# Weight halves in the attention stages: low halves on VectorE, all high halves on ScalarE, none on GpSimd

## The chip, the cores and the metric

One NeuronCore of a Trainium2 chip runs the whole kernel. The metric is device time in microseconds (us): the median of three runs, 1567.07 us for the kernel before (1562.07 to 1567.22). One execution was also profiled, and it took 1567.67 us, of which the profile's span covers 1564.4 us.

The engines carry the names of the profile. PE is TensorE (matrix products), DVE is VectorE, ACT is ScalarE, POOL is GpSimd and SP issues the loads. Each engine works through its own queue in order. An instruction that waits holds up all that stands behind it on its engine, and nothing on the others unless they need its result.

## The reference, cut to what matters

Three blocks run one after the other on a sequence of 512 tokens (16 more in front in the first block): a recurrent mixer with a gated MLP, the hybrid attention block with cross attention into 256 memory tokens, and a squared-ReLU MLP. The change touches the second block:

```python
def hybrid_mixer(h, w_in, g_group, sinks, w_out, rel_table):
    proj = (h @ w_in).astype(jnp.float32)
    ...
    ya = dilated_attention(heads(aq), heads(ak), heads(av), rel_table)
    yb = stick_breaking_attention(heads(bq), heads(bk), heads(bv))
    yc = sliding_window_sink_attention(heads(cq), heads(ck), heads(cv), sinks, rel_table)
    yd = moba_attention(heads(dq), heads(dk), heads(dv), rel_table)
    groups = []
    for y in (ya, yb, yc, yd):
        y = y.transpose(0, 2, 1, 3).reshape(B, S, -1)
        groups.append(y * lax.rsqrt(jnp.mean(y * y, axis=-1, keepdims=True) + NORM_EPS))
    y = jnp.concatenate(groups, axis=-1) * g_group.astype(jnp.float32)
    return y.astype(h.dtype) @ w_out
```

Four groups (A, B, C, D) of four heads with 64 features each share one input projection and one output projection. Behind them comes the cross attention with its own query, key, value and output weights.

## The kernel before, in words

The features stand on the 128 partitions and the tokens along the free axis. A product with fp32 accuracy is made from pairs: each operand is held as a high half and a low half in a reduced format, and PE makes three products (high with high, high with low, low with high). `weights` (line 112) fetches one 128x1024 piece of weights into the staging tile `wst` (SP queue, three buffers), makes the high half `whi` by a rounding copy, and makes the low half `wlo` by subtracting `whi` from `wst`. `whi` and `wlo` have three buffers each; the matmuls of lines 135 to 138, 165 to 168 and 1349 to 1352 read them. Each piece is asked for while the product in front of it is being made.

Who makes the halves is set by `self.wlow` and a counter `self.turns`. Over most of the kernel `wlow` is VectorE: ACT makes `whi` (line 125) and DVE makes `wlo` (line 126). In two places `wlow` is GpSimd: while the heads of the four groups are woven with the projections (line 1524 to 1527), and in the cross attention (line 1621 to 1717). There POOL makes every `wlo` (line 126), and `whi` is made in turns by DVE (line 123) and ACT (line 125).

The weave (line 1270) takes the heads as generators, advances them in turn and puts pieces of the projections between them. A head of group B makes scores (line 1231), masks its diagonal block on POOL (lines 1238 and 1252), splits on ACT and DVE (lines 106, 107, 1255, 1256) and multiplies into the values. The softmax heads of A, C and D make scores (1162), an exponential (1174), a scaling by the denominator (1180), transposes (1184) and a split from PSUM (106, 107). Queries and keys are evacuated on DVE (1354) and split by ACT and DVE (1119, 1120, 1131 to 1134). In the cross attention the residual `x` takes the output projection (1641), and `split_x` makes its halves on ACT (109) and DVE (110) and adds squares on POOL (241).

The order on each engine is not the order of the source: the framework's scheduler sets it when the program is built, from its own model of how long each instruction takes.

Of the kernel before, what the change touches and what calls it, by code (L numbers as in the profile page):

```python
# [11 lines left out]
FT = mybir.dt.float32  # L12
FR = mybir.dt.float32r
AF = mybir.ActivationFunctionType
OP = mybir.AluOpType
# [48 lines left out]
class Net:  # L64
    def __init__(self, ctx, tc, I, out, dump=None):
        self.ctx, self.tc, self.nc, self.I, self.out = ctx, tc, tc.nc, I, out
        self.dump = dump
        nc = self.nc
        ent = lambda name, bufs=1, space=None: ctx.enter_context(
            tc.tile_pool(name=name, bufs=bufs) if space is None else tc.tile_pool(name=name, bufs=bufs, space=space))  # L70
        self.const = ent("const")
        self.wst = ent("wst", 3)
        self.whi = ent("whi", 3)
        self.wlo = ent("wlo", 3)
        self.act = ent("act")
        self.nrm = ent("nrm")
        self.dram = ent("dram", 1, DR)
        self.pmx, self.turn, self.third = None, 0, 0
        self.wlow, self.turns = nc.vector, 0
        self.pmm = ent("pmm", 2, PS)  # L80

        c = self.const
        self.ident = c.tile([P, P], FT, name="ident")
        make_identity(nc, self.ident)
        self.ones = c.tile([P, P], FT, name="ones")
        nc.vector.memset(self.ones, 1.0)
        self.ones2 = c.tile([P, 2], FR, name="ones2")
        nc.vector.tensor_copy(self.ones2, self.ones[:, 0:2])
        self.eps = c.tile([P, 1], FT, name="eps")
        nc.vector.memset(self.eps, EPS)  # L90
        self.par = c.tile([P, NPAR], FT, name="par")
        nc.sync.dma_start(self.par, I["par"])
        self.tri = c.tile([P, P], FT, name="tri")
        nc.gpsimd.affine_select(self.tri, self.ones, pattern=[[1, P]], compare_op=OP.is_ge, fill=0.0, base=0,
                                channel_multiplier=-1)
# [16 lines left out]
    def weights(self, src, shape, own=None):  # L112

        nc = self.nc
        kt, cols = shape
        n = kt * cols
        st = self.wst.tile([P, 1024], FT, name="wst")
        nc.sync.dma_start(st[:, 0:n] if len(src.shape) == 2 else st[:, 0:n].rearrange("p (k c) -> p k c", k=src.shape[1]),
                          src)
        hi, lo = ((own or self.whi).tile([P, 1024], FR, name="whi"), (own or self.wlo).tile([P, 1024], FR, name="wlo"))  # L120
        self.turns += 1
        if self.wlow is nc.gpsimd and self.turns % 2:
            nc.vector.tensor_copy(hi[:, 0:n], st[:, 0:n])
        else:
            nc.scalar.activation(hi[:, 0:n], st[:, 0:n], AF.Copy)  # L125
        self.wlow.tensor_tensor(lo[:, 0:n], st[:, 0:n], hi[:, 0:n].bitcast(FT), OP.subtract)  # L126
        v = lambda t: t[:, 0:n].rearrange("p (k c) -> p k c", k=kt)
        return v(hi), v(lo)

# [1168 lines left out]
    def hybrid(self):  # L1298
        nc = self.nc
        V = nc.vector  # L1300
        I = self.I
        with ExitStack() as es:
# [129 lines left out]
            def heads(name, j):  # L1432
                def gens():
                    box = boxes[name]
                    g = "ABCD".index(name)
                    if name == "C":
                        yield from band_heads(j)
                        return
                    for i in range(2):
                        h = 2 * j + i  # L1440
                        y, yr, q = ys[2 * g + j], slice(64 * i, 64 * i + 64), box["q", j][i]
                        if name == "B":
                            yield from self.stick_units(q, box["k", j][i], box["v"], 64 * h, y, yr)
                            continue
                        e = self.bias_tile({"A": 0, "D": 8}[name] + h)
                        yield from self.softmax_units(lambda pair, q=q: (q, 256 * pair), box["k", j][i], box["v"],
                                                      64 * h, y, yr, causal, e)
                return gens
# [49 lines left out]
            def expand(jobs):  # L1498

                res = []  # L1500
                for job in jobs:
                    nxt = flat[order[id(job)] + 1:][:1]
                    steps = list(job[1])
                    if job is plan[0][1][-1]:
                        res += steps[:-1] + [lambda nx=nxt[0][0], s0=steps[-1]: (nx(), s0())]
                        continue
                    if nxt and nxt[0][0]:
                        s0 = steps[0]
                        steps[0] = lambda s0=s0, nx=nxt[0][0]: (nx(), s0())
                    res += steps  # L1510
                return res
# [9 lines left out]
            e3.close()  # L1521
            self.at = self.pool(e2, "at", 6)
            self.ap = self.pool(e2, "ap", 1)
            self.wlow = nc.gpsimd
            self.vx = self.pool(e2, "vx", 1)
            self.weave([(heads(*hs), expand(jobs)) for hs, jobs in plan[1:]])
            self.wlow = V
            if self.dump:
                for n in range(KT):
                    self.dump("y" + "ABCD"[n // 2], n % 2, ys[n])  # L1530
# [76 lines left out]
    def cross(self, es, out):  # L1607

        nc = self.nc
        V = nc.vector  # L1610
# [7 lines left out]
        self.qk = self.pool(es, "qk3", 6)  # L1618
        self.at = self.pool(es, "at3", 4)
        self.ap = self.pool(es, "ap3", 1)  # L1620
        self.wlow = nc.gpsimd
        self.me = self.pool(self.ctx, "mlpe", side="right")
        self.hid = []
        self.next_input(act2)
# [89 lines left out]
        for _, pieces in mups:  # L1714
            for piece in pieces[3:6]:
                piece()
        self.wlow = V

    def mlp_up(self, f, pool, tmp, ranges, own=None):

# [210 lines left out]
```

## Time and profile before

| what | value |
|---|---|
| median of the runs | 1567.07 us |
| the profiled execution / its span | 1567.67 us / 1564.4 us |
| PE busy | 1479.6 us (95%) |
| DVE busy | 1032.0 us (66%) |
| ACT busy | 724.1 us (46%) |
| POOL busy | 335.5 us (21%) |
| POOL on `wlo`, line 126 | 75.2 us, 34 instructions |

The shares are means over the whole span. The 34 `wlo` of POOL all lie between 876 and 1165 us, so a view of that stretch says more than the page: the busy time of each engine in it, the groups of instructions by line and shape with the mean time of one, the shortest, the middle and the longest instruction of a line, and the chain of waits, which goes back from the last instruction to what released each step.

### The profile page before, as it was taken

What the parts mean: (1) busy time and instruction counts of PE and PEld (TensorE: products, weight loads), DVE (VectorE), ACT (ScalarE), POOL (GpSimd) and SP (SyncE); (2) the same over time, 40 slices, a digit from 0 to 9 for tenths busy, and PEclk for the clock granted to TensorE, in tenths of its full rate; (3) what the DMA queues carried; (4) which work ended last, traced back from release to release, by engine and by line L of the source; (5) the groups of instructions that cost most, each with busy time, mean ns of one, the idle gap of its engine ahead of it and who ended that gap; (6) DMA issues with size and microseconds to landing.
All of it is one profiled execution on the core that took longest, in us unless ns stands there. A gap on an engine that the chain in (4) does not pass through costs nothing.

```text
span 1564.4 us, 25002 instructions
## 1 busy us (share of the span) xinstructions
PE 1479.6 (95%) x9761; PEld 1334.2 (85%) x9761; DVE 1032.0 (66%) x1968; ACT 724.1 (46%) x1400; POOL 335.5 (21%) x308
## 2 busy tenths in 40 slices
PE   5998999999989999999999999999789999999997
PEld 4988999988989899999999877877778888888886
DVE  8887879777577655555475878888887443344334
ACT  5233356664554433334455466575666431134332
POOL 4066721003342000000131445303342000000001
PEclk9998999999999999999999999999999999999998
DMA  5333232227444322223656222113220322333221
GB/s 189 96 98 105 80 120 75 64 74 234 148 136 135 95 93 93 90 95 118 187 152 217 78 67 68 55 44 125 90 81 32 93 95 93 96 94 96 93 94 54
DMA packets 66430, 161.95 MB, mean 104 GB/s; under 512 B 15100, under 2 KB 24556, under 8 KB 66184
## 3 DMA queue, kind: packets, MB, share of 16 engines
q1 hardware_dynamic: 64936, 157.74, 32.3%
q8 instruction: 76, 1.25, 0.3%
q0 software_dynamic: 288, 1.57, 0.3%
q10 hardware_dynamic: 1088, 1.05, 0.2%
q14 instruction: 42, 0.34, 0.1%
HBM read 153.92 MB, written 10.33 MB: 105 GB/s over the span
## 4 chain that ended last, share of the span: by engine, by line
PE 54%; DVE 10%; ACT 3%; issue 1%; DMA 1%; POOL 0%; DVEq 0%; ACTq 0%; POOLq 0%
PE mm L135 6%; PE mm L138 5%; PE mm L136 5%; PE mm L165 5%; PE mm L168 5%; PE mm L167 5%; PE mx L165 4%; PE mx L168 4%; PE mx L167 4%; DVE xl L110 2%; PE mx L135 2%; PE mx L138 2%; PE mx L136 2%; DVE ptl L107 1%; PE tr L1208 1%
## 5 line engine op out<-in xcount | busy, mean ns | idle before, releaser
L126 DVE TENSOR_TENSOR wlo<-wst,whi 128x1024 fp32r<-128x1024 f32 (+2 forms) x227 | 285.0, 1257 | 196.9 <-ACT whi L125 121.2
L125 ACT ACTIVATE whi<-wst 128x1024 fp32r<-128x1024 f32 (+3 forms) x244 | 251.9, 1034 | 302.9 <-PE mm L136 107.3
L168 PE MATMUL mm<-xl,whi 128*128 128x256 f32 (+4 forms) x808 | 233.5, 314 | 0.3 <-DVE xl L110 0.3
L167 PE MATMUL mm<-xh,whi 128*128 128x256 f32 (+4 forms) x808 | 233.1, 314 | 0.2 <-DVE x L1641 0.2
L167 PE MATMUL mx<-xh,whi 128*128 128x512 f32 (+4 forms) x552 | 170.6, 330 | 7.8 <-ACT xh L109 7.7
L168 PE MATMUL mx<-xl,whi 128*128 128x512 f32 (+4 forms) x552 | 170.9, 330 | 3.3 <-DVE xl L110 3.2
L167 PEld LDWEIGHTS mm<-xh,whi 128*128 128x128 f32 (+1 forms) x808 | 153.8, 190 | 9.9 <-DVE x L1670 0.3
L168 PEld LDWEIGHTS mm<-xl,whi 128*128 128x128 f32 (+1 forms) x808 | 153.3, 190 | 10.3 <-issue 0.6
L165 PE MATMUL mm<-xh,wlo 128*128 128x256 f32 (+4 forms) x808 | 139.2, 311 | 0.0
L135 PE MATMUL mm<-hh,whi 128*128 128x256 f32 (+1 forms) x496 | 139.2, 310 | 0.0
L136 PE MATMUL mm<-hl,whi 128*128 128x256 f32 (+1 forms) x496 | 139.0, 310 | 0.0
L165 PEld LDWEIGHTS mm<-xh,wlo 128*128 128x128 f32 (+1 forms) x808 | 116.4, 187 | 9.8 <-issue 0.5
L167 PEld LDWEIGHTS mx<-xh,whi 128*128 128x128 f32 (+1 forms) x552 | 105.8, 192 | 17.1 <-ACT xh L109 8.0
L168 PEld LDWEIGHTS mx<-xl,whi 128*128 128x128 f32 (+1 forms) x552 | 105.6, 191 | 14.3 <-DVE xl L110 4.9
L165 PE MATMUL mx<-xh,wlo 128*128 128x512 f32 (+4 forms) x552 | 104.6, 331 | 0.0
L126 POOL TENSOR_TENSOR wlo<-wst,whi 128x1024 fp32r<-128x1024 f32 (+1 forms) x34 | 75.2, 2217 | 120.5 <-PE mm L138 38.2
L993 POOL TENSOR_TENSOR acc<-acc,osq 128x256 f32<-128x256 f32 (+1 forms) x26 | 25.2, 969 | 344.6 <-ACT osq L990 344.6
L135 PEld LDWEIGHTS mm<-hh,whi 128*128 128x128 f32 x496 | 93.4, 188 | 6.1
L136 PEld LDWEIGHTS mm<-hl,whi 128*128 128x128 f32 x496 | 93.5, 189 | 5.8
L165 PEld LDWEIGHTS mx<-xh,wlo 128*128 128x128 f32 (+1 forms) x552 | 85.5, 193 | 9.4 <-issue 0.2
L138 PE MATMUL mm<-hh,wlo 128*128 128x256 f32 (+1 forms) x496 | 83.6, 310 | 1.9 <-DVE wlo L126 1.9
L138 PEld LDWEIGHTS mm<-hh,wlo 128*128 128x128 f32 x496 | 70.5, 188 | 8.0 <-DVE wlo L126 2.3
(553 smaller groups left out, 3353.3 us busy)
## 6 DMA issues: line engine op xcount, KB each, us to landing
wst<-in_w_in_dram SPq DMA_DIRECT2D x52, 512.0 KB, 3.6
wst<-in_w_down_dram SPq DMA_DIRECT2D x32, 512.0 KB, 3.5
wst<-in_w_mup_dram SPq DMA_DIRECT2D x32, 512.0 KB, 3.5
wst<-in_w_mdown_dram SPq DMA_DIRECT2D x32, 512.0 KB, 3.7
wst<-in_w_gate_dram SPq DMA_DIRECT2D x22, 512.0 KB, 3.5
wst<-in_w_up_dram SPq DMA_DIRECT2D x22, 512.0 KB, 3.6
wst<-in_w_out_dram SPq DMA_DIRECT2D x20, 512.0 KB, 3.6
wst<-in_w_down_dram SPq DMA_DIRECT2D x16, 384.0 KB, 3.5
```

Source lines behind the costliest of these rows:

```text
L107: nc.vector.tensor_tensor(lo, src, hi.bitcast(FT), OP.subtract)
L110: nc.vector.scalar_tensor_tensor(lo, src, gain, hi.bitcast(FT), OP.mult, OP.subtract)
L125: nc.scalar.activation(hi[:, 0:n], st[:, 0:n], AF.Copy)
L126: self.wlow.tensor_tensor(lo[:, 0:n], st[:, 0:n], hi[:, 0:n].bitcast(FT), OP.subtract)
L135: nc.tensor.matmul(ps, ah, bh, start=start and i == 0, stop=False)
L136: nc.tensor.matmul(ps, ah, bl, start=False, stop=False)
L138: nc.tensor.matmul(ps, al, bh, start=False, stop=stop and i == n - 1)
L165: nc.tensor.matmul(ps, wl[:, k], xh, start=False, stop=k == KT - 1)
L167: nc.tensor.matmul(ps, wh[:, k], xh, start=k == 0, stop=False)
L168: nc.tensor.matmul(ps, wh[:, k], xl, start=False, stop=False)
L993: nc.gpsimd.tensor_tensor(acc, acc, sq, OP.add)
L1208: nc.tensor.matmul(yp[0:64, c0:c1], m[:, j, vc:vc + 64], d[:, j - f0, c0:c1], start=ji == x == 0, stop=ji == len(jobs) - 1 and x == 2)
```

## The change

`self.wlow` and `self.turns` go. Everywhere in the kernel ACT makes `whi` and DVE makes `wlo`, as before the change outside of the two stretches. By the alternation 17 of the 34 `whi` of these stretches were made on DVE (13 of 1024 columns, 4 of 512); they move to ACT. The 34 `wlo` (26 of 1024 columns, 8 of 512) move from POOL to DVE.

```diff
@@ -76,7 +76,6 @@
         self.pmx, self.turn, self.third = None, 0, 0
-        self.wlow, self.turns = nc.vector, 0
         self.pmm = ent("pmm", 2, PS)
@@ -118,12 +117,8 @@
         hi, lo = ((own or self.whi).tile([P, 1024], FR, name="whi"), (own or self.wlo).tile([P, 1024], FR, name="wlo"))
-        self.turns += 1
-        if self.wlow is nc.gpsimd and self.turns % 2:
-            nc.vector.tensor_copy(hi[:, 0:n], st[:, 0:n])
-        else:
-            nc.scalar.activation(hi[:, 0:n], st[:, 0:n], AF.Copy)
-        self.wlow.tensor_tensor(lo[:, 0:n], st[:, 0:n], hi[:, 0:n].bitcast(FT), OP.subtract)
+        nc.scalar.activation(hi[:, 0:n], st[:, 0:n], AF.Copy)
+        nc.vector.tensor_tensor(lo[:, 0:n], st[:, 0:n], hi[:, 0:n].bitcast(FT), OP.subtract)
@@ -1521,10 +1516,8 @@
             self.ap = self.pool(e2, "ap", 1)
-            self.wlow = nc.gpsimd
             self.vx = self.pool(e2, "vx", 1)
             self.weave([(heads(*hs), expand(jobs)) for hs, jobs in plan[1:]])
-            self.wlow = V
@@ -1618,7 +1611,6 @@
         self.ap = self.pool(es, "ap3", 1)
-        self.wlow = nc.gpsimd
@@ -1714,7 +1706,6 @@
                 piece()
-        self.wlow = V
```

Line numbers of the changed kernel are 5 lower from line 126 on (line 126 becomes 121) and 8 lower in the cross attention (1641 becomes 1633).

The scheduler also moves other instructions. POOL's queue in the stage of the B heads, first before; `e` is a diagonal block of scores, masked by `strict`:

```order
L1238 TENSOR_TENSOR e_10463<-e_10463,strict_9967 128x128
L1252 TENSOR_TENSOR e_10484<-e_10484,strict_9967 128x128
L126 TENSOR_TENSOR wlo_10777<-wst_10774,whi_10776 128x1024
L1238 TENSOR_TENSOR e_10496<-e_10496,strict_9967 128x128
L126 TENSOR_TENSOR wlo_10931<-wst_10928,whi_10930 128x1024
L1252 TENSOR_TENSOR e_10526<-e_10526,strict_9967 128x128
```

The same place of POOL's queue in the changed kernel:

```order
L1233 TENSOR_TENSOR e_10463<-e_10463,strict_9967 128x128
L1247 TENSOR_TENSOR e_10484<-e_10484,strict_9967 128x128
L1233 TENSOR_TENSOR e_10496<-e_10496,strict_9967 128x128
L1247 TENSOR_TENSOR e_10526<-e_10526,strict_9967 128x128
L1233 TENSOR_TENSOR e_10540<-e_10540,strict_9967 128x128
```

The masks no longer stand behind a `wlo`. The two `wlo` of these rows are now in DVE's queue, here between pieces of the B heads (`ptl` is the low half of a block, `v2l` that of the values):

```order
L1232 SCALAR_TENSOR_TENSOR e_10496<-tr_10493,e_10496 128x512
L1251 TENSOR_TENSOR ptl0_10517<-e_10484,pth0_10516 128x256
L121 TENSOR_TENSOR wlo_10777<-wst_10774,whi_10776 128x1024
L109 SCALAR_TENSOR_TENSOR v2l_10409<-mm_10715,rc272_10186,v2h_10408 128x256
L121 TENSOR_TENSOR wlo_10931<-wst_10928,whi_10930 128x1024
L106 TENSOR_TENSOR ptl1_10400<-e_10496,pth1_10399 128x512
```

The `ptl1` of 512 columns now waits for both. The second place is the start of the cross attention on DVE, where `x` takes the output projection from PSUM. Before:

```order
L1641 TENSOR_TENSOR x0_5046<-x0_5046,mm_13154 128x256
L1641 TENSOR_TENSOR x1_5048<-x1_5048,mm_13171 128x256
L123 CAST whi_13217<-wst_13215 128x1024
L110 SCALAR_TENSOR_TENSOR xl0_13126<-x0_5046,par_89,xh0_13118 128x256
L123 CAST whi_13286<-wst_13284 128x1024
L110 SCALAR_TENSOR_TENSOR xl1_13127<-x1_5048,par_89,xh1_13119 128x256
L1641 TENSOR_TENSOR x2_5050<-x2_5050,mm_13196 128x256
L1641 TENSOR_TENSOR x3_5052<-x3_5052,mm_13221 128x256
```

The same place in the changed kernel:

```order
L1633 TENSOR_TENSOR x0_5046<-x0_5046,mm_13154 128x256
L1633 TENSOR_TENSOR x1_5048<-x1_5048,mm_13171 128x256
L109 SCALAR_TENSOR_TENSOR xl0_13126<-x0_5046,par_89,xh0_13118 128x256
L109 SCALAR_TENSOR_TENSOR xl1_13127<-x1_5048,par_89,xh1_13119 128x256
L1633 TENSOR_TENSOR x2_5050<-x2_5050,mm_13196 128x256
L121 TENSOR_TENSOR wlo_13218<-wst_13215,whi_13217 128x1024
L1633 TENSOR_TENSOR x3_5052<-x3_5052,mm_13221 128x256
L121 TENSOR_TENSOR wlo_13262<-wst_13259,whi_13261 128x1024
L121 TENSOR_TENSOR wlo_13287<-wst_13284,whi_13286 128x1024
L1633 TENSOR_TENSOR x4_5054<-x4_5054,mm_13240 128x256
```

Two `whi` went to ACT's queue and three `wlo` came in, of which two stand between the evacuations of `x3` and `x4`.

## Rows read from the trace of the kernel before

**Rows 1.** Busy time of each engine in a stretch (us from the span's start; length; busy us and instructions of PE, PEld, DVE, ACT, POOL; granted clock, DMA share, GB/s). The first stretch lies in the first block, where DVE makes the `wlo`; the second is the attention.

```profile
200.00:300.00 100.00, 100.00 (x816) 94.48 (x815) 85.50 (x170) 62.17 (x130) 15.38 (x17) 1.00 0.28 87
876.00:1200.00 324.00, 295.01 (x1930) 260.26 (x1929) 268.15 (x647) 201.61 (x534) 117.22 (x96) 0.98 0.22 71
```

**Rows 2.** POOL's groups by line and shape in 876 to 1200 us: count, busy us, mean ns of one, idle us of POOL just before them and what ended it.

```profile
L126 POOL TENSOR_TENSOR wlo<-wst,whi 128x1024 fp32r<-128x1024 f32 x26 | 64.4, 2480 | 61.0 <-PE tr L1208 24.1 <-ACT whi L125 16.0 <-DVE whi L123 6.2
...
L126 POOL TENSOR_TENSOR wlo<-wst,whi 128x512 fp32r<-128x512 f32 x8 | 10.8, 1361 | 59.5 <-PE mm L138 36.0 <-PE mm L1349 9.1 <-DVE qs L1120 7.1
```

**Rows 3.** Instructions of POOL and of DVE in order of time around 890 us: start us, us, engine, line.

```profile
890.13 2.59 POOL L126 TENSOR_TENSOR wlo<-wst,whi 128x1024 fp32r<-128x1024 f32 x1 [5.95 <-PE mm L1349]
...
888.71 0.68 DVE L1133 TENSOR_TENSOR kl<-qkn,kh 64x512 fp32r<-64x512 f32 x1 [0.37 <-ACT kh L1131]
...
890.93 2.33 DVE L1133 TENSOR_TENSOR kl<-qkn,kh 64x512 fp32r<-64x512 f32 x1
```

**Rows 4.** The low half of a block of scores, DVE line 107, read from PSUM (`tr`) and from SBUF (`e`), in 876 to 1165 us: shortest/middle/longest ns, first and last start.

```profile
L107 DVE TENSOR_TENSOR ptl<-tr,pth x53: 278/418/692, 1003.6 to 1164.8; 128x256 fp32r<-128x256 f32 x25, 128x128 fp32r<-128x128 f32 x12, 128x384 fp32r<-128x384 f32 x8, 128x512 fp32r<-128x512 f32 x8
L107 DVE TENSOR_TENSOR ptl<-e,pth x16: 292/558/2569, 904.5 to 985.7; 128x128 fp32r<-128x128 f32 x4, 128x256 fp32r<-128x256 f32 x4, 128x384 fp32r<-128x384 f32 x4, 128x512 fp32r<-128x512 f32 x4
```

**Rows 5.** DVE's groups by line and shape in 876 to 1200 us, as in rows 2.

```profile
L110 DVE SCALAR_TENSOR_TENSOR xl<-x,par,xh 128x256 fp32r<-128x256 f32 x33 | 27.6, 844 | 2.1 <-ACT xh L109 2.1
...
L1120 DVE TENSOR_TENSOR qs<-qkn,qs 64x512 fp32r<-64x512 f32 x16 | 13.1, 816 | 1.1 <-ACT qs L1119 0.6
L123 DVE CAST whi<-wst 128x1024 fp32r<-128x1024 f32 x13 | 12.3, 946 | 2.1 <-PE mm L136 2.1
L1133 DVE TENSOR_TENSOR kl<-qkn,kh 64x512 fp32r<-64x512 f32 x14 | 12.1, 866 | 3.0 <-ACT kh L1131 2.9
...
L126 DVE TENSOR_TENSOR wlo<-wst,whi 128x1024 fp32r<-128x1024 f32 x3 | 5.0, 1660 | 3.6 <-ACT whi L125 2.7 <-issue 0.8
L1256 DVE TENSOR_TENSOR ptl<-e,pth 128x512 fp32r<-128x512 f32 x4 | 5.0, 1239 | 0.1
```

**Rows 6.** Shortest/middle/longest ns of lines of DVE, as in rows 4; the row of line 126 is of the whole span (its list of shapes names three of more), and the last row says how long DVE sat idle before its 227 `wlo` until ACT's `whi` was there (us, times).

```profile
L110 DVE SCALAR_TENSOR_TENSOR xl<-x,par,xh x19: 469/774/2586, 875.4 to 1158.3; 128x256 fp32r<-128x256 f32 x19
L1133 DVE TENSOR_TENSOR kl<-qkn,kh x14: 674/689/2325, 888.7 to 1035.0; 64x512 fp32r<-64x512 f32 x14
L123 DVE CAST whi<-wst x17: 420/685/2897, 889.3 to 1160.8; 128x1024 fp32r<-128x1024 f32 x13, 128x512 fp32r<-128x512 f32 x4
L107 DVE TENSOR_TENSOR xl<-y,xh x6: 681/686/687, 1046.8 to 1103.3; 128x512 fp32r<-128x512 f32 x6
L1180 DVE TENSOR_SCALAR e<-e,den x8: 340/344/836, 1170.7 to 1182.7; 128x256 f32<-128x256 f32 x8
L1178 DVE TENSOR_TENSOR den<-den,es x16: 140/152/1459, 1065.1 to 1106.4; 128x1 f32<-128x1 f32 x16
L126 DVE TENSOR_TENSOR wlo<-wst,whi x227: 949/1225/2535, 6.9 to 1533.6; 128x1024 fp32r<-128x1024 f32 x105, 128x768 fp32r<-128x768 f32 x8, 128x64 fp32r<-128x64 f32 x1
...
  ACT whi L125: 121.2, 72
```

**Rows 7.** The chain of waits in 876 to 1200 us: start us, us, what. The first and the last of its 229 DVE pieces, and of the fourteen long ones among them six, the first and the last included.

```profile
887.58 0.44 DVE qkn L1354
...
890.93 2.34 DVE kl L1133
...
927.15 2.17 DVE ptl L107
...
1113.50 2.81 DVE whi L123
...
1118.09 4.13 DVE xl L110 x2
...
1155.21 2.54 DVE wlo L126
...
1161.64 2.73 DVE e L1180 x2
...
1184.65 1.33 DVE xl L110 x2
```

**Rows 8.** The first and the last of the 76 ACT pieces of the same chain.

```profile
887.16 0.39 ACT rs L294
...
1167.84 0.28 ACT pth L106
```

**Rows 9.** ACT's groups by line and shape in 876 to 1200 us, as in rows 2.

```profile
L125 ACT ACTIVATE whi<-wst 128x1024 fp32r<-128x1024 f32 x17 | 17.7, 1054 | 5.5 <-PE mm L138 4.0 <-PE mm L136 0.8 <-PE mm L1352 0.4
...
L125 ACT ACTIVATE whi<-wst 128x512 fp32r<-128x512 f32 x4 | 2.5, 630 | 2.7 <-POOL wlo L126 2.7
```

**Rows 10.** Who waited for whom in 876 to 1200 us: us in total, times, longest. The first and the last of the eight waits of PE for DVE, and one of ACT for POOL.

```profile
PE mm L135 <- DVE x L1641: 4.4, 4, 2.0
...
PE tr L1263 <- DVE ptl L1256: 1.0, 1, 1.0
...
ACT pth L106 <- POOL e L1238: 7.3, 10, 2.1
```

**Rows 11.** POOL's masks of the B heads and its sums of squares in 876 to 1200 us, shortest/middle/longest ns.

```profile
L1238 POOL TENSOR_TENSOR e<-e,strict x16: 455/540/969, 903.7 to 982.5; 128x128 f32<-128x128 f32 x16
...
L241 POOL TENSOR_TENSOR nacc<-nacc,sq x28: 727/778/1704, 875.3 to 1199.1; 128x256 f32<-128x256 f32 x28
```

## The prediction

> **What bounds the kernel now.** First comes the busy time by stretch [rows 1]. The change lies in the attention, 324 us from 876 to 1200 us. There PE is busy for 295.0 us, so it idles for 29.0 us, and DVE is busy for 268.2 us, or 83%. In the stretch of the first block PE is busy throughout, with DVE at 85.5% and DVE making the `wlo` there: a DVE that is this full need not stop PE.
>
> Then come POOL's groups [rows 2]. Its 34 `wlo` take 64.4 + 10.8 = 75.2 us, and POOL sits idle for 61.0 + 59.5 = 120.5 us before them. Read alone, this is an idle engine that takes work from a full one.
>
> The third view shows its price. At 890.13 us POOL begins a `wlo` of 2.59 us. A `kl` on DVE that begins at 890.93 takes 2.33 us and ends within 0.6 us of POOL's end, while the `kl` of the same form at 888.71 took 0.68 [rows 3]. Line 107 shows which instructions are hit: 53 that read one operand from PSUM never take over 0.69 us, and 16 of the same shapes that read both operands from SBUF take up to 2.57 [rows 4]. So a DVE instruction with two SBUF operands stands still while POOL makes a `wlo`. A cast from SBUF does too: at worst it takes 2.90 us and in the middle 0.69 [rows 6].
>
> The groups tell how much this is [rows 5, 6]: `xl` 27.6 - 33 x 0.47 = 12.1 us, `qs` 13.1 - 16 x 0.69 = 2.1, the cast 12.3 - 13 x 0.685 = 3.4, `kl` 12.1 - 14 x 0.69 = 2.4, `ptl` of 512 columns 5.0 - 4 x 0.69 = 2.2. That is 22 us in five groups alone, a few of them under POOL's smaller work.
>
> Last comes the chain of waits: 229 of its pieces in the attention are DVE's [rows 7], 123 us together, which is 46% of DVE's 268.2 busy. ACT has 76 pieces [rows 8] with 35.8 us, 18% of its 201.6.
>
> **The change part by part.** *The stall of DVE goes.* Fourteen DVE pieces of the chain between 890.93 and 1161.64 lie under a `wlo` of POOL and are over 1.3 us long [rows 7]; they add up to 34.2 us. Undisturbed, by the middle or shortest durations of rows 6, they are 0.69 each for one `kl`, one `qs`, five low or high halves of scores and one cast, 0.15 for a denominator, 0.47 for each of four `xl`, 1.23 for a `wlo` and 0.34 for each of two scalings, 9.5 together. Charging 0.69 for every half of scores, whatever its width, is on the safe side. So 34.2 - 9.5 = 24.7 us of stall stand on the chain. The bounds: 0, if another chain is always as late, and 29.0, all that PE idles [rows 1].
>
> *The low halves come to DVE.* 26 of 1024 columns at 1.225 us [rows 6] make 31.9 us, 8 of 512 columns at 0.686, as the `xl` of the same shape, make 5.5. The casts that leave are 13 x 0.685 + 4 x 0.42 = 10.6 us. Net, 37.4 - 10.6 = 26.8 us are added to DVE. On the path it is between 0 and all of it; I take DVE's share on the chain, 46%, since the new instructions stand between others of DVE: 12.3 us.
>
> *The high halves come to ACT.* 13 x 1.054 + 4 x 0.63 = 16.2 us [rows 9]. ACT is busy for 62% of the stretch; at its share of the chain, 18%, this is 2.9 us (bounds 0 and 16.2).
>
> *POOL's queue is shorter.* The masks of the B heads stood behind `wlo`, and ACT waited for them ten times, 7.3 us [rows 10]. At ACT's 18% this gives 1.3 us back (bounds 0 and 7.3). The loads of `xk` and `xv` that POOL issues also stand behind no `wlo` any more; I cost that at nothing. The staging buffers come free when DVE has read them, after 1.2 us and not 2.5, so SP can issue a load earlier; its queue moves a few loads of weights and bias past each other, and the rows name no wait for a load, so I cost this at nothing; a load that came late would cost its own lateness on the path.
>
> *New waits.* A `wlo` on DVE needs ACT's `whi`, the landed load and a free buffer. Behind it on DVE wait the evacuations and halves that follow, and PE for those; at the start of the cross attention two `wlo` stand between the evacuations of `x3` and `x4`. The casts that stood in the same places waited 2.1 us in all [rows 5], but a cast needs no other engine's half. I put nothing in the sum for it, and keep it as the first rival.
>
> The sum, against the profiled execution: 24.7 + 1.3 - 12.3 - 2.9 = 10.8 us less, 1567.67 - 10.8 = 1556.9. The median of the runs, 1567.07, is 0.6 lower than that execution, which doesn't matter here. I forecast 1557 us; for this case alone 1550 to 1564.
>
> A rule of the Trainium skill speaks against the change. Perfetto Trace Analysis, Optimizing Scalar/DVE Operations, says that with VectorE saturated it may make sense to give work to ScalarE or even GpSimd, and adds that between VectorE and GpSimd this might not help, as they share a read port. Its first half would have POOL's 75.2 us as a relief; this trace bears out the second half, with at least 22 us of stall in five groups, more than half of the 37.4 us that POOL takes over.
>
> **The rivals.** *DVE waits in line, slower.* POOL could afford to sit idle 120.5 us before its `wlo`; DVE can't. For it: in this kernel 72 of DVE's 227 `wlo` waited for ACT's `whi`, 121.2 us, 1.7 each [rows 6], and one of the three in this stretch waited 2.7 [rows 5]. Against it: those 72 are of the whole kernel and come to 0.5 us for each `wlo`, and the longest of POOL's waits were for PE (36.0 us for line 138 alone, rows 2), for buffers that a product frees with its end, whose evacuation now stands ahead of the `wlo` on DVE. If DVE inherits 48 us, two fifths, at 46% this costs 22 us: 1579. From 23 us on it eats up the gain, from 40 on the kernel is slower.
>
> *PE is right behind, no change.* The 24.7 us are stall on the chain, and it says nothing of the next latest. PE waited for DVE eight times in the list, 4.4 us down to 1.0, 18.2 together [rows 10]. If only these can shrink, then by the stall's share of the chain's DVE pieces, 24.7 of 123 or 20%, less the 10% that the net new work adds: 1.8 us, 1566. Against it: the chain goes through ACT and DVE in ways that PE's idle alone doesn't show.
>
> *More than the sum.* The stall off the chain counts too, and all 18.2 us of PE's waits for DVE go: 1549. For it speaks that all of the `wlo` work is shorter on DVE than the pair of POOL's work and stall; against it, that DVE stays at some 75%.
>
> *DVE now holds POOL up.* What reads two SBUF operands on DVE can also delay POOL: the longest mask takes 0.97 us and the shortest 0.46, the longest sum 1.70 and the shortest 0.73 [rows 11]. Some 13 of the new `wlo` stand among the B heads; at up to 1.23 us each this makes 16 us for the masks, and, at ACT's 18%, 2.9 us of the time: about 1560.
>
> Such a lock is what the Trainium skill states in SBUF — State Buffer, SBUF: two separate sides: of the two engines the one that starts first has the shared pair for its whole instruction and the other blocks. By that rule the stall would only change sides; the masks' and sums' longest times agree that POOL is held as well.
>
> **How the numbers follow.** The forecast has 0.46, the larger gain 0.11, PE right behind 0.17, the held POOL 0.07, DVE in line 0.19. About 0.5% is what can be told from no change here: 1559.2 to 1574.9. Of the forecast's 0.46, 0.36 lie below 1559.2, since the stalls under 1.3 us were not counted; with the larger gain faster has 0.47. The other 0.10, PE right behind and the held POOL make 0.34. Slower is the line on DVE, 0.19. The range has to leave 0.1 out on either side: below the larger gain's 1549 and into the upper half of the line on DVE, so 1547 to 1578.
>
> **What will show it.** In the attention POOL's busy time falls from 117 to about 42 us, and ACT's rises from 202 to about 218. The low halves of scores with both operands in SBUF no longer take over 1.2 us, and `xl` has a middle near 0.47. DVE's busy time doesn't rise though it has 26.8 us more to do; if it rises by that much, the stall was no stall. PE's idle of 29.0 us falls by some 10. The forecast is wrong if DVE's idle time before its new `wlo` comes to more than 23 us, or if PE's idle is the same in spite of a DVE that has become free.

## The result: 0.7% faster, and the profile after

The changed kernel takes 1553.45 us (median of 4 runs, 1551.67 to 1556.99) against 1566.24 us for the kernel before (4 runs): 0.9929 of its time, interval 0.9908 to 0.9949. Measured once more, later, the same kernel came to 0.9916 (0.9903 to 0.9928). The forecast was 1557 us, with 10.8 us of gain; by the first ratio it is 11 us, by the second 13.

The page of the changed kernel begins with the busy time of each engine, over the whole span:

```profile
span 1554.9 us, 24997 instructions
PE 1481.5 (95%) x9761; PEld 1337.3 (86%) x9761; DVE 1013.2 (65%) x1985; ACT 737.4 (47%) x1417; POOL 259.7 (17%) x274
```

In the kernel before, DVE was busy for 1032.0 us, 18.8 more, although by the prediction's count it has 26.8 us more to do now. Together that is some 45 us of stall that is gone, an estimate from these two numbers.

The attention as one stretch, as in [rows 1] (ten us shorter, since the kernel is):

```profile
876.00:1190.00 314.00, 295.02 (x1936) 261.24 (x1935) 250.99 (x665) 215.65 (x553) 42.59 (x64) 0.98 0.23 73
```

PE has the same 295.0 us to do and idles for 19.0 instead of 29.0. DVE's groups by line and shape in this stretch (count, busy us, mean ns, idle us before them and what ended it) answer to [rows 5]:

```profile
L121 DVE TENSOR_TENSOR wlo<-wst,whi 128x1024 fp32r<-128x1024 f32 x29 | 35.4, 1226 | 4.8 <-ACT whi L120 3.6 <-PE mm L1344 0.9
L109 DVE SCALAR_TENSOR_TENSOR xl<-x,par,xh 128x256 fp32r<-128x256 f32 x34 | 21.2, 633 | 1.1 <-ACT xh L108 1.0
...
L1115 DVE TENSOR_TENSOR qs<-qkn,qs 64x512 fp32r<-64x512 f32 x16 | 11.1, 696 | 1.9 <-ACT qs L1114 1.4
L1128 DVE TENSOR_TENSOR kl<-qkn,kh 64x512 fp32r<-64x512 f32 x14 | 9.6, 682 | 0.9 <-ACT kh L1126 0.6
```

The means of `qs` and `kl` fell from 816 and 866 ns to 696 and 682, which were the middle values before. Shortest, middle and longest of line 106 (107 before), of `xl` and of POOL's mask, to be read beside [rows 4], [rows 6] and [rows 11]:

```profile
L106 DVE TENSOR_TENSOR ptl<-e,pth x16: 280/488/694, 903.9 to 979.4; 128x128 fp32r<-128x128 f32 x4, 128x256 fp32r<-128x256 f32 x4, 128x384 fp32r<-128x384 f32 x4, 128x512 fp32r<-128x512 f32 x4
...
L109 DVE SCALAR_TENSOR_TENSOR xl<-x,par,xh x26: 468/582/958, 872.8 to 1164.3; 128x256 fp32r<-128x256 f32 x26
...
L1233 POOL TENSOR_TENSOR e<-e,strict x16: 458/463/975, 903.1 to 978.2; 128x128 f32<-128x128 f32 x16
```

A low half of scores with both operands in SBUF took up to 2569 ns before and takes at most 694 now. The middle `xl`, 582 ns, still stands above its undisturbed 0.47 us: POOL's sums of squares run beside it, and in a kernel below that makes these sums on DVE the middle is 477 ns.

Who waited for whom after the change (us in total, times, longest), as in [rows 10]:

```profile
ACT pth L105 <- POOL e L1233: 6.8, 7, 2.1
...
PE tr L1258 <- DVE pth L1250: 1.4, 1, 1.4
...
PE mm L130 <- DVE qkn L1349: 0.9, 1, 0.9
```

The first row is nearly that of before, 7.3 us. The other two come back below: they lie close together in one place, and there the kernel before waited too, 1.6 us for `qkn` and 1.0 for `ptl` (the last PE row of [rows 10]). The chain of waits of the same stretch, by line:

```profile
by line: PE mm L1347 8.1%; PE mm L1346 8.0%; PE mm L1344 8.0%; PE tr L1203 6.3%; PE mm L133 6.1%; PE mm L130 6.1%; PE mm L131 5.7%; PE sc L1157 3.4%; DVE xl L109 3.2%; PE tr L1179 3.0%; DVE wlo L121 2.4%; PE tr L1258 2.1%; DVE ptl L106 2.0%
```

The low halves are 2.4% of 314 us of chain, 7.5 us, out of 40.9 us (35.4 and eight of 512 columns) that they keep DVE busy. Over all lines the chain's DVE pieces add up to some 60 us; they were 123.

### The profile page after: what moved, and what is told of

Same layout as the page of the kernel before. It is cut to its first block, busy times and chain, and to the rows that moved or that the text cites. A ratio compares the mean times of both kernels' runs of the same rounds, so it can differ in the third digit from the quotient of the medians.

```text
span 1554.9 us, 24997 instructions
## 1 busy us (share of the span) xinstructions
PE 1481.5 (95%) x9761; PEld 1337.3 (86%) x9761; DVE 1013.2 (65%) x1985; ACT 737.4 (47%) x1417; POOL 259.7 (17%) x274
## 4 chain that ended last, share of the span: by engine, by line
PE 60%; DVE 6%; ACT 2%; DMA 1%; issue 0%; DVEq 0%; ACTq 0%
PE mm L130 6%; PE mm L133 6%; PE mm L131 6%; PE mm L160 5%; PE mm L163 5%; PE mm L162 5%; PE mx L160 4%; PE mx L163 4%; PE mx L162 4%; PE mx L130 2%; PE mx L133 2%; PE mx L131 2%; PE mm L1347 2%; PE mm L1346 2%; PE mm L1344 2%; PE tr L1203 1%
## 5 line engine op out<-in xcount | busy, mean ns | idle before, releaser
L121 DVE TENSOR_TENSOR wlo<-wst,whi 128x1024 fp32r<-128x1024 f32 (+2 forms) x261 | 320.9, 1231 | 201.4 <-ACT whi L120 122.6
L120 ACT ACTIVATE whi<-wst 128x1024 fp32r<-128x1024 f32 (+2 forms) x261 | 267.9, 1028 | 306.3 <-PE mm L131 114.7
L236 POOL TENSOR_TENSOR nacc<-nacc,sq 128x256 f32<-128x256 f32 (+2 forms) x62 | 59.9, 967 | 208.9 <-ACT sq L235 202.6
```

The lines of the kernel that those rows point to most:

```text
L121: nc.vector.tensor_tensor(lo[:, 0:n], st[:, 0:n], hi[:, 0:n].bitcast(FT), OP.subtract)
L236: (nc.vector if k % len(accs) else nc.gpsimd).tensor_tensor(acc[:, c:c + w], acc[:, c:c + w], sq, OP.add)
```

## The experiments

**One half of the change at a time.** In the first kernel DVE makes the low halves and the high halves go on in turns; in the second ACT makes all high halves and POOL keeps the low ones.

```diff
-        self.wlow.tensor_tensor(lo[:, 0:n], st[:, 0:n], hi[:, 0:n].bitcast(FT), OP.subtract)
+        nc.vector.tensor_tensor(lo[:, 0:n], st[:, 0:n], hi[:, 0:n].bitcast(FT), OP.subtract)
```

> Half of the change alone: all low halves on VectorE, the high halves in turns on VectorE and ScalarE as before. Theory A (the gain is the stall of VectorE under GpSimd's low halves, now gone): the casts stay, 10.6 us on VectorE at 46% cost 4.9 us against the changed kernel's 1553.5, ScalarE is spared 16.2 us at 18%, 2.9 us back: about 1555 us, nearly the whole gain. Rival B (the gain is the casts that left VectorE): 1562 to 1566 us, near the kernel before.

```diff
-        self.turns += 1
-        if self.wlow is nc.gpsimd and self.turns % 2:
-            nc.vector.tensor_copy(hi[:, 0:n], st[:, 0:n])
-        else:
-            nc.scalar.activation(hi[:, 0:n], st[:, 0:n], AF.Copy)
+        nc.scalar.activation(hi[:, 0:n], st[:, 0:n], AF.Copy)
```

> The other half alone: all high halves on ScalarE, the low halves of the attention stay on GpSimd. Theory A: the stall stays, the casts' 10.6 us leave VectorE (4.9 us less on the path) and 16.2 us come to ScalarE (2.9 more): about 1564 us, no change that can be told from before. The instructions of VectorE with two SBUF operands still take up to 2.5 us. Rival B: about 1555 us.

Low halves alone: 1550.08 us, 0.9899 (0.9880 to 0.9917). High halves alone: 1564.47, 0.9998 (0.9984 to 1.0012). The whole gain comes with the low halves. The page of the second kernel is the more telling one:

```profile
span 1561.7 us, 25004 instructions
PE 1479.5 (95%) x9761; PEld 1333.6 (85%) x9761; DVE 1013.8 (65%) x1951; ACT 737.1 (47%) x1417; POOL 331.5 (21%) x308
```

DVE and ACT are busy for the same time as in the changed kernel, within 0.6 us, and no gain can be told: here DVE's time still holds the stall, there it holds work that could wait. Line 107 in this kernel, `ptl<-e,pth`, still takes up to 1694 ns.

**POOL's work brought back as a ghost.** The changed kernel, with one instruction added behind each low half of the attention: POOL makes the same subtraction once more, in place in the staging tile, where nobody reads it. Once it is of full width, once of 64 columns. The two have the same instructions, but not the same order: from 913 us on, the scheduler gave DVE, ACT and PE their work in another sequence. So the pair compares POOL's time together with the order that was built around it; the expectation of the second ghost, written before, takes the places to be the same.

```diff
         nc.vector.tensor_tensor(lo[:, 0:n], st[:, 0:n], hi[:, 0:n].bitcast(FT), OP.subtract)
+        if self.ghost:
+            m = min(n, 1024)       # 64 in the second kernel
+            nc.gpsimd.tensor_tensor(st[:, 0:m], st[:, 0:m], hi[:, 0:m].bitcast(FT), OP.subtract)
```

> The changed kernel, and in the attention GpSimd makes each low half once more, in place in the staging tile, where nobody reads it (34 instructions of 1024 or 512 columns; the results are not touched). Theory A: GpSimd is busy for some 75 us more, VectorE's instructions with two SBUF operands again take up to 2.6 us, VectorE's busy time in the attention rises by some 45 us, and the time by the 24.7 us that were counted on the chain: about 1578 us, at least 1566, though nothing waits for these results but the staging buffers. Rival C (the gain is that GpSimd's queue is empty for the masks): about 1558 us, and the next run loses as much as this one.

> As the run before it, with GpSimd's additional instruction cut to 64 columns: the same 34 instructions with the same dependences and places, but a short time on the port. Theory A: VectorE's longest instructions stay under 1.5 us, and the time is within 4 us of the changed kernel's 1553.5. Rival C: about 1558 us, as the full one. If the staging buffers that are held longer were the cost, this one would lose some of what the full one loses.

Full width: 1592.74 us, 1.0172 (1.0151 to 1.0193). 64 columns: 1555.14, 0.9937 (0.9920 to 0.9953). So 37.6 us hang on POOL's time and on what the scheduler made of it; the expectation was a loss of 24.7. Groups of POOL and of DVE with the full ghost, 876 to 1235 us:

```profile
L125 POOL TENSOR_TENSOR wst<-wst,whi 128x1024 f32<-128x1024 f32 x26 | 65.0, 2501 | 63.0 <-DVE wlo L122 38.6 <-DVE rst L282 7.5 <-DVE den L1178 5.7
...
L122 DVE TENSOR_TENSOR wlo<-wst,whi 128x1024 fp32r<-128x1024 f32 x30 | 44.1, 1468 | 4.1 <-ACT whi L121 3.3 <-ACT e L1170 0.6
L1119 DVE TENSOR_TENSOR qs<-qkn,qs 64x512 fp32r<-64x512 f32 x16 | 16.8, 1050 | 2.2 <-ACT qs L1118 1.8
L1132 DVE TENSOR_TENSOR kl<-qkn,kh 64x512 fp32r<-64x512 f32 x14 | 14.7, 1051 | 0.9 <-ACT kh L1130 0.6
```

and with the ghost of 64 columns:

```profile
L125 POOL TENSOR_TENSOR wst<-wst,whi 128x64 f32<-128x64 f32 x34 | 16.1, 473 | 159.2 <-DVE wlo L122 79.5 <-DVE den L1178 44.2 <-issue 19.2
...
L1119 DVE TENSOR_TENSOR qs<-qkn,qs 64x512 fp32r<-64x512 f32 x16 | 11.2, 698 | 1.9 <-ACT qs L1118 1.4
L1132 DVE TENSOR_TENSOR kl<-qkn,kh 64x512 fp32r<-64x512 f32 x14 | 9.6, 683 | 0.9 <-ACT kh L1130 0.6
```

A `kl` that has nothing to do with the ghost takes 1051 ns on average beside the long one and 683 beside the short one. The ghost could also do harm in another way: it holds the staging tile longer and stands ahead of the masks. But `whi` waited for the ghost in the staging tile for 2.7 us with the long one and 2.9 with the short, no engine waited for a load in this stretch with the long one, and the masks held ACT up for 6.8 us in both. That leaves the stall and the order. How much stall lies on the chain of waits can be counted: the time by which a DVE instruction on the chain exceeds the middle duration of its form in the kernels without long POOL work, while a `wlo` or a ghost runs on POOL. This estimate comes to 37 us with the long ghost and to nothing with the short one; it is some 27 us in the kernel before and nothing in the changed one. So the stall that the long ghost puts on the chain is about as large as the loss. That the other order costs nothing of its own is not shown.

The Trainium skill states a lock between the two engines: whichever of them starts first keeps the shared port pair for its whole instruction, and the other one waits (SBUF — State Buffer, SBUF: two separate sides). The 1051 ns against 683 agree with it.

Where the 37.6 us are lost shows in two windows (start and end, length, busy us and count of PE, PEld, DVE, ACT, POOL, granted clock, DMA share, GB/s): from the first B score to the start of the cross attention, and from there to its end. With the long ghost:

```profile
901.30:1133.70 232.40, 209.12 (x1230) 177.64 (x1229) 198.71 (x465) 146.08 (x376) 70.61 (x57) 0.94 0.22 66
1133.70:1232.90 99.20, 83.97 (x576) 77.66 (x576) 82.24 (x180) 59.72 (x159) 40.73 (x35) 0.88 0.20 65
```

and with the short one:

```profile
894.60:1107.90 213.30, 202.47 (x1229) 175.93 (x1228) 166.36 (x461) 146.39 (x376) 27.33 (x57) 0.96 0.23 70
1107.90:1189.30 81.40, 75.40 (x577) 69.09 (x577) 70.88 (x179) 58.82 (x159) 25.94 (x35) 1.00 0.25 79
```

DVE is busy for 281.0 us against 237.2 with the same work. PE's idle time is 38.5 us with the long ghost and 16.8 with the short, and PE's busy time 293.1 and 277.9, at granted clocks of 0.94 and 0.88 in the two stages against 0.96 and 1.00. So some 22 us are waits, and 15 us are a PE that takes longer for the same products at a lower granted clock.

**One stage at a time.** The full change only while the heads are woven (first B score to the first `x<-x,mm` of line 1641), and only in the cross attention (from there to the last one of line 1670). The third kernel gives the heads the low halves on DVE but keeps the turns, and leaves the cross attention as before.

```diff
@@ heads only: against the kernel before
-            self.wlow = nc.gpsimd
             self.vx = self.pool(e2, "vx", 1)
@@ cross only: against the kernel before
-        self.wlow = nc.gpsimd
         self.me = self.pool(self.ctx, "mlpe", side="right")
@@ heads, low halves alone: against the kernel before
-        self.wlow.tensor_tensor(lo[:, 0:n], ...
+        self.wlo_on.tensor_tensor(lo[:, 0:n], ...      # GpSimd in the cross attention alone
```

> The change in the stage of the heads alone; the cross attention stays as before. Theory A, with the pieces of the chain: 13 us of stall go there, 1.3 for the masks, against 8.6 for the low halves less the casts and 1.9 for the high halves at the shares of the prediction: 4 us less than before, about 1562 us. If planned work on VectorE costs less than those shares say (the run with the low halves alone came out below the changed kernel), 1556 to 1560.

> The change in the cross attention alone; the stage of the heads stays as before. Theory A: 11.6 us of stall on the chain go there, against 3.6 and 0.9: 7 us less than before, about 1559 us, and with the run of the other stage the two gains add up to that of the whole change within 3 us. If they don't add up, the order that the scheduler found for the whole is a cause of its own.

> Low halves on VectorE in the stage of the heads alone, high halves in turns everywhere, the cross attention as before. In the stage of the heads both halves of the change together gave nothing (0.9993 of before). Theory A with ScalarE as the price there: the stall that goes is worth some 3 to 4 us and the high halves on ScalarE took it back, so this run is 1560 us against 1563.5. Rival D (PE is right behind in that stage whatever VectorE does): 1563 us, as with both halves.

Heads only: 1563.25 us, 0.9993 (0.9980 to 1.0007), no gain where 4 us were expected. Cross only: 1553.75, 0.9922 (0.9902 to 0.9942), 12 us where 7 were expected. The two add up to what the whole change gave, within 3 us. Heads with the low halves alone: 1556.49, 0.9938 (0.9922 to 0.9953), 10 us where 3 to 4 were expected. So there was a gain to be had in the heads, and in the kernels that make all high halves on ACT there it is gone again. The two stages as windows, first of the kernel before:

```profile
896.30:1111.50 215.20, 199.99 (x1232) 171.81 (x1231) 178.47 (x450) 136.18 (x364) 70.12 (x57) 0.98 0.22 69
1111.50:1200.50 89.00, 75.99 (x576) 70.67 (x575) 75.85 (x177) 56.18 (x155) 40.53 (x35) 0.98 0.22 72
```

of the changed kernel:

```profile
898.80:1110.50 211.70, 200.26 (x1230) 173.66 (x1229) 165.64 (x462) 146.33 (x376) 16.60 (x32) 0.98 0.23 70
1110.50:1191.00 80.50, 74.63 (x576) 68.83 (x575) 70.16 (x180) 58.69 (x159) 23.54 (x28) 1.00 0.25 79
```

of the heads with the full change alone, and with the low halves alone:

```profile
892.60:1109.10 216.50, 205.44 (x1229) 178.59 (x1228) 167.15 (x459) 145.66 (x375) 23.84 (x35) 0.94 0.23 69
```

```profile
893.50:1101.70 208.20, 198.24 (x1229) 170.24 (x1228) 171.94 (x472) 136.41 (x364) 26.45 (x35) 0.99 0.23 72
```

The cross attention is 8.5 us shorter: PE idles 5.9 us there and not 13.0. In the heads the full change lowers PE's idle time (11.1 and 11.4 us, from 15.2), but PE takes longer for the same products: 205.44 us at a clock of 0.94, where the low halves alone have 198.24 at 0.99. These are single profiles: of two kernels that were profiled twice, the changed one and the low halves alone, the heads agree within 1.7 us and the cross attentions within 0.6.

**Small parts on top of the low halves.** With the first kernel's edit, the sums of squares of the attention on DVE, and in another the two masks of the B heads (lines 1238 and 1252) on DVE.

```diff
@@ sums
-            (nc.vector if k % len(accs) else nc.gpsimd).tensor_tensor(acc[:, c:c + w], acc[:, c:c + w], sq, OP.add)
+            (nc.vector if k % len(accs) or self.wlow is nc.gpsimd else nc.gpsimd).tensor_tensor(acc[:, c:c + w], acc[:, c:c + w], sq, OP.add)
@@ masks
-            G.tensor_tensor(e[:, 0:P], e[:, 0:P], self.strict, OP.mult)
+            V.tensor_tensor(e[:, 0:P], e[:, 0:P], self.strict, OP.mult)
```

> Low halves on VectorE with high halves in turns (the best so far, 1550.1), and in both stages the sums of squares go from GpSimd to VectorE too. Theory A: the stall of some 7 us that VectorE's halves of x still have under these sums goes, against 28 sums at 0.41 us, 11.5 us, that the scheduler can place: if planned work costs its full time, 4 us slower (1554); if stall on the chain costs more than work that has a place in the order, 2 to 4 us faster (1546 to 1548).

> Low halves on VectorE with high halves in turns, and the 32 masks of the B heads go from GpSimd to VectorE. They take 0.46 us and two changes of engine on GpSimd, and some 0.29 us on VectorE, 9.3 us in all; the waits of ScalarE and VectorE for the masks, some 10 us, go. Theory A has nearly no stall to remove here (the masks are short): within 3 us of 1550.1. If the changes of engine on the path of the B heads are a cost, 1545 to 1547.

Sums: 1549.39 us, 0.9899 (0.9882 to 0.9917), as without them. The middle `xl` falls from 556 to 477 ns, and DVE has the sums to make; either the two balance or neither lies on the path, which this run doesn't tell. Masks: 0.9919 (0.9899 to 0.9940), no gain either, although ACT's waits for them could have gone.

**The change and its low half again, on one chip.** The changed kernel and the first kernel, unedited.

> The changed kernel once more, on the same chip as the next run, to tell the two apart: 1553.5 us as before. If ScalarE's 16.2 us of high halves cost some time, the next run is 0.2 to 0.4% below this one; if they are hidden, within 0.1%.

> Low halves on VectorE with high halves in turns, once more beside the changed kernel: 1550 us and 0.3% below it, if the high halves on ScalarE cost what the first comparison showed; the same as it, if that was chance.

1552.92 us, 0.9916 (0.9903 to 0.9928), and 1551.24, 0.9910 (0.9896 to 0.9924). The two can't be told apart by their times here; the 0.3% between them at first came from two separate measurements and was not found again. What differs is where they lose. Their heads take 213.4 and 209.7 us, their cross attentions 80.5 and 82.9.

**One cast back on DVE.** Ten us at a time, the heads of the changed kernel show one place where PE's clock falls:

```profile
960.00:970.00 10.00, 10.00 (x55) 8.47 (x54) 5.21 (x12) 5.85 (x15) 1.85 (x4) 1.00 0.19 59
970.00:980.00 10.00, 7.67 (x44) 7.01 (x43) 8.22 (x14) 6.55 (x14) 2.17 (x4) 0.76 0.18 52
980.00:990.00 10.00, 10.00 (x72) 9.59 (x72) 5.72 (x22) 4.31 (x13) 0.92 (x2) 0.90 0.01 2
```

and DVE in order of time (start us, us, engine, line), with one `whi` of ACT ahead of it, shows what stands there:

```profile
968.65 1.06 ACT L120 ACTIVATE whi<-wst 128x1024 fp32r<-128x1024 f32 x1
...
970.92 0.29 DVE L1243 TENSOR_SCALAR e<-sc 128x128 f32<-128x128 f32 x1 [1.56 <-PE sc L1240]
971.25 1.23 DVE L121 TENSOR_TENSOR wlo<-wst,whi 128x1024 fp32r<-128x1024 f32 x1
972.51 0.69 DVE L1128 TENSOR_TENSOR kl<-qkn,kh 64x512 fp32r<-64x512 f32 x1
973.23 0.69 DVE L1115 TENSOR_TENSOR qs<-qkn,qs 64x512 fp32r<-64x512 f32 x1
973.95 0.57 DVE L1250 CAST pth<-e 128x512 fp32r<-128x512 f32 x1
...
975.18 1.29 DVE L1349 SCALAR_TENSOR_TENSOR qkn<-mm,rs 128x512 f32<-128x512 f32 x2
```

DVE waits 1.56 us for PE, and then a `wlo` of 1.23 us stands ahead of `pth` and `qkn`, for which PE waits 1.42 and 0.92 us. Its `whi` was ready at 969.7, so it could have filled most of that wait. The changed kernel in both profiles, the one with the heads alone and the one with the short ghost show this pair of waits (1.4, and 0.9 or 0.7 us); with the long ghost PE waits here at other instructions. The kernels with the low halves on DVE and the high halves in turns don't show it (the one with the masks on DVE has three other waits near it, 1.3 us together). The kernel before does wait here, 1.0 us for `ptl` [rows 10] and

```profile
PE mm L135 <- DVE qkn L1354: 1.6, 1, 1.6
```

with a clock of 0.98 and 0.85 in the two tens from 970 on. So the full change did not bring this loss: it keeps most of it, where the low halves alone shed it. One high half given back to DVE makes the scheduler order this place otherwise:

```diff
+        self.piece += 1            # set to 0 ahead of the weave
+        if self.piece == 10:
+            nc.vector.tensor_copy(hi[:, 0:n], st[:, 0:n])
+        else:
+            nc.scalar.activation(hi[:, 0:n], st[:, 0:n], AF.Copy)
-        nc.scalar.activation(hi[:, 0:n], st[:, 0:n], AF.Copy)
```

> The full change, but the tenth piece of weights that the heads ask for has its high half made by DVE (one cast of 0.69 us); all other high halves stay on ACT. By the order that is built, this moves instructions only around 945 to 1000 us: the low half that stood at 971.25 in the changed kernel now stands ahead of the part of scores for which DVE waited 1.56 us for PE, and the split of the B head and the halves of queries and keys no longer stand behind it. Theory 1 (place): in the changed kernel PE waited 1.42 + 0.92 us there and the granted clock fell to 0.76 in 970 to 980 us; all four kernels with all high halves on ACT in the heads and low halves on DVE show such a wait of 2.3 to 2.4 us between 965 and 976, and the three with turns there show none. Then this wait goes, the clock stays at 1.00 from 960 to 990, the stage of the heads is 206.5 to 209.5 us long instead of 211.7 to 213.4, and the time is 1547 to 1550, 0.988 to 0.9905 of the kernel before. Theory 2 (amount): the heads lose because ACT makes some ten high halves more; one of them less changes under 1.1 us: the stage stays at 210.6 to 213.4, the time at 1552 to 1554, 0.991 to 0.993. If the wait goes and the time stays, PE loses it again later in the stage, and the place was not the cause.

1548.28 us (1546.52 to 1549.10), 0.9894 (0.9870 to 0.9918): the lowest ratio of the study, though low halves alone (0.9899 and 0.9910) can't be told from it. Its heads, and the same place:

```profile
895.30:1102.70 207.40, 197.09 (x1229) 170.42 (x1228) 165.34 (x462) 146.03 (x375) 16.72 (x32) 0.99 0.23 72
...
970.00:980.00 10.00, 8.70 (x67) 8.08 (x68) 7.83 (x20) 6.76 (x18) 2.83 (x5) 1.00 0.12 48
980.00:990.00 10.00, 10.00 (x76) 9.45 (x75) 8.89 (x28) 7.31 (x18) 0.46 (x1) 1.00 0.09 26
```

The heads take 207.4 us with ACT as busy as before (146.0), so the amount of work on ACT was not what cost them. Theory 1 fits, with one correction: the wait didn't go, it shrank from 2.34 to 1.48 us (0.78 and 0.70). PE's clock stayed at 1.00, and that is most of the gain: against the changed kernel PE is busy for 3.2 us less and idle for 1.1 less. The run moves some dozens of instructions between 945 and 1047 us, farther than the expectation says, so it points to the order around this place and doesn't show that this one `wlo` did it. That it beats the changed kernel rests on its heads and on ratios from different chips whose intervals overlap.

## Why the prediction was right, and where its terms were off

- **The stall of DVE goes (24.7 us).** Right in kind: the long durations left with POOL's `wlo` and came back with the long ghost. No run measures this term by itself. The count over the chain gives some 27 us for the kernel before, close to the 24.7, and 37 us for the long ghost, on a DVE that also makes the low halves. So the price is no constant of POOL's work; that it grows with how full DVE is would fit, but two cases don't show it.
- **The low halves on DVE (46% of them on the path).** This term was mis-sized. The 46% was the share of DVE's busy time that lay on a chain which the stall itself had drawn through DVE. With the stall gone, 7.5 of 40.9 us lie on the chain, 18%. By the prediction's steps the low halves alone (24.7 - 0.46 x 37.4 + 1.3) would have given 8.8 us; they gave 14 to 16.
- **The high halves on ACT (2.9 us, against 4.9 that the casts leave free).** By these steps a gain of 2.0; high halves alone gave 0.3 within 2 us either way, which does not rule the 2.0 out; on top of the low halves they gave nothing (1553 us with them, 1551 without, on one chip). In the cross attention they helped (80.5 us against 82.3 and 82.9 with turns), in the heads they cost as much or more (211.7 and 213.4 against 209.8 and 209.7), and the run with one cast back points to the order around 970 us. The prediction cost moved order at nothing. The errors of this term and of the one before have opposite signs. That the sum came out right to a few us is in part luck.
- **The masks (1.3 us).** Wrong: ACT's wait for them is 6.8 us and was 7.3, and masks on DVE gain nothing. They wait for what feeds them: POOL sat idle for 40.8 us before the masks of line 1233 until DVE's `e` was there.
- **New waits (nothing).** DVE's idle time before its `wlo` by releaser comes to some 10 us, far from the 23 that the first rival needed:

```profile
  ACT whi L120: 5.0, 7
  issue: 1.8, 1
  PE mm L1344: 1.7, 2
  ACT hh L105: 1.1, 1
```

  The rival was wrong as a sum but not as a mechanism: at one place work did stand in line behind a `wlo`. Loads, also cost at nothing, held engines up for 1.4 us there (0.8 for a staging tile, 0.6 for `bias`), and for 0.3 before.
- **PE is right behind.** Wrong, for the heads too. There the full change alone gives 0.9993, as this rival would have it, but the low halves alone give 0.9938: PE was not what stood in the way. The 18.2 us that the rival starts from are the eight largest groups of PE's waits for DVE, not eight waits; all groups together make 22.4, which changes its 1.8 us to 2.2.
- **DVE holds POOL up.** Right as a mechanism, wrong as a sum. The longest mask is 975 ns, as before (969), and it ends 0.32 us after a `kl` on DVE that began just ahead of it; the shortest mask takes 0.46 us in all:

```profile
958.61 0.68 DVE L1128 TENSOR_TENSOR kl<-qkn,kh 64x512 fp32r<-64x512 f32 x1
958.64 0.97 POOL L1233 TENSOR_TENSOR e<-e,strict 128x128 f32<-128x128 f32 x1 [3.39 <-DVE e L1232]
```

  But all 32 masks together stand 2.1 us above 0.46 each, where the rival counted 16; before it was 3.8 us.
- **What was to be seen.** POOL's 42.6 us, ACT's 215.7, the longest `ptl`, DVE's falling busy time and PE's idle time (10 us less) came as written; only `xl`, with 0.58 for 0.47, did not.

## What to carry to other kernels

When a slow engine works beside a busy one, don't count only the work that it takes over: look in the busy one for the same instruction with two durations, and at what the other engine does during the long ones. The price of moving work is not its share of the chain before, because the chain changes with it; and a gain in one stretch can be gone in the next kernel's order, so look at each stretch by itself. Where a scheduler sets the order, a change of engine moves instructions that have nothing to do with it: here another order of the heads went with some 4 us, about a third of what the change gave.

## What was not expected of the hardware

The same 1013 us of DVE (1013.2 and 1013.8) went with times 11 us apart. And short waits of PE went with more lost time than their own: around 2.34 us of waits in 970 to 980 us the granted clock fell from 1.00 to 0.76, a mix of the two levels of 2.4 and 1.2 GHz, and was back at 1.00 after 990; around 1.48 us, cut into two, it stayed at 1.00, while with the masks on DVE three waits of 1.3 us together went with 0.83 in 960 to 970 us. With the heads changed alone, where the same pair of waits came at 966 to 970 us, the ten us behind it ran at 0.72:

```profile
960.00:970.00 10.00, 7.66 (x44) 6.32 (x43) 7.09 (x14) 7.72 (x17) 1.85 (x4) 0.94 0.18 54
970.00:980.00 10.00, 10.00 (x59) 9.66 (x59) 5.44 (x16) 3.88 (x10) 1.80 (x4) 0.72 0.01 2
```

It isn't the idle time alone that decides: in the kernel with the low halves alone in the heads, PE was busy for only 7.67 us of 1080 to 1090 us and 7.74 us of the next ten, and the clock stayed at 1.00 in both. What makes the difference stays open.
